# An encoder layer on one core: tiles 0 to 3 turned with a lag of two, norms issued behind a duo's splits, the latents' sums in other buffers and without GpSimd

## The chip, the core and the metric

The kernel runs on one core of a Trainium2 chip. A core has five engines with a queue each: PE (TensorE, the matrix engine), DVE (VectorE), ACT (ScalarE), POOL (GpSimd) and SP, which only issues DMAs here. An engine works through its queue in order; instructions of different engines wait for each other by semaphores. The metric is the device time of one execution in microseconds (us), less is better. The kernel before takes 2342.51 us, the median of three runs (2338.19 to 2344.05).

## The reference, cut to what matters

One layer over 1024 tokens of width 1024, in float32, with four layer norms (LN1 to LN4):

```
x  <- LN1(a*x + 0.5*SwiGLU_1(x))
proj = x @ w_in      -> q_lat (384), kv_lat (256), k_rope (32), u (512), gates g_a, g_b
y_a = attention(q = rms_norm(q_lat) w_uq, k, v = rms_norm(kv_lat) w_uk, w_uv) w_o_attn
y_b = (z * sigmoid(z w_glu)) w_o_ssm,   z = gelu(s5_forward(u) + s5_backward(u) + d*u)
x  <- LN2(a*x + (sigmoid(g_a)*y_a + sigmoid(g_b)*y_b) w_out)
x  <- LN3(a*x + 0.5*SwiGLU_2(x))
x  <- LN4(a*x + sigmoid(x w_pg) * (p w_pp))

rms_norm(t, g) = t * rsqrt(mean(t*t) + 1e-6) * g
layer_norm(t)  = (t - mean) * rsqrt(var + 1e-5) * g + b
SwiGLU(x)      = (silu(x w1) * (x w3)) w2,  w1, w3: 1024 x 2816, w2: 2816 x 1024
```

## The kernel before, in words

**Precision and splits.** A float32 product is made of three matmuls of a shorter type: each operand is split into a high part `hi` (ACT copies and rounds, line 64) and a low part `lo = x - hi` (DVE subtracts, line 65), and hi*hi, hi*lo and lo*hi are added in PSUM. So nearly every operand of PE costs one ACT copy and then one DVE subtraction, in this order (`split`). Names ending in hi, h and lo, l are such halves.

**Feed-forward down (`ffn_down`).** The product with w2 is a block scheme of seven stages; the last is stage 4. A stage goes through the 22 chunks of w2 in six *duos* (two chunks, the last has one). For a duo the hidden values (`hh`, `hl`) and the weights (`wh`, `wl`) are split, then PE does 24 matmuls of 128x512 into four accumulators `pd` (line 441), four for each of the six pairs (rows of token tile t, 128 tokens each). Token tiles 0 to 3 are complete before stage 4 starts, and their layer norm is done within it: in the duo with q = 1 to 4 the generator yields tile q-1 after that duo's splits are written in the program. Tiles 4 to 7 are complete after the last duo.

**Norm and turn (`norm_in`, `layer_norm`, `transpose_in`).** Each yielded tile is normed (ACT: a Square over 128x1024 into `scr`, line 123, and a Sqrt, line 125; DVE: eight 128x1 operations, lines 120 to 130, and two of 128x1024 on `acc`, lines 133 and 135). When more than `lag` normed tiles are waiting, the oldest is turned: eight 128x128 transposes on PE into `tln` (line 148), then a split into `xhi`, `xlo`. `finish` turns those left over. The lag is 4 for LN1 and LN3 and 4 (with blocks) for LN2. After LN1 comes the product with w_u (`pu`), whose moving operand is four turned tiles wide; after LN3 comes the gate of the last layer norm (`pgate`), one tile at a time.

**Latents (`latents`).** Chunks 0 to 2 (q) and 3, 4 (kv) of x w_lat are squared (ACT, line 617), added (DVE, line 619), split, and summed over partitions by a matmul with ones (`pms`, lines 624 and 625), for two halves of 512 tokens. DVE and ACT make the root and its reciprocal (627, 629, 630), and four POOL operations of 128x512 refine it (a Newton step, lines 631 to 634). That is done four times (two groups, two halves). The 128x512 scratch tiles carry the tags t0 to t3, Xr and Xi of the S5 branch's pool; S5's parameter chain on POOL and DVE (line 1104, tiles of 128x32 and their multiples) uses the slots of t2, t3 and Xr too. PE meanwhile does the gates' projection (`pg`).

**Behind S5.** The latents come back from memory (`lat`), POOL multiplies them by the reciprocal root (line 858), ACT scales by the gain and rounds (859), and DVE makes the low part (860) into `ckl` and `mx`. Beside it run the gated linear unit of S5 (`pglu`, `sg`, `sl`), and then the keys (`pk`) and queries (`pq`).

**Order.** The program is written as one list; a scheduler places each engine's instructions by their dependences and buffers, so an edit at one place can reorder an engine's queue around it. `tc.issue_after(x)` binds what is issued in it behind instruction x. Buffers are slots of a tag: a tile whose slot is still in use waits for the last user.

## Time and profile before

| | |
|---|---|
| median of three runs | 2342.51 us |
| profiled execution, its own time | 2340.56 us |
| its span, first to last instruction | 2338.7 us |
| PE busy | 2260.9 us, 97% |
| DVE busy | 1547.1 us, 66% |
| ACT busy | 968.9 us, 41% |
| POOL busy | 269.5 us, 12% |

The profile shows one execution. PE is busy for 97% of the span, so the span less PE's busy time, 77.8 us, is what all its waits, the start and the tail together take. A matmul of 128x512 follows the one before in 0.23 us at a granted clock of 2.4 GHz, and in 0.43 us where the throttle grants 1.2 GHz; a matmul's own duration is longer, since they overlap. A row of the timeline reads: start, duration, engine, line, operation, output <- inputs, shape, count, and in brackets the idle time of that engine just before it with what ended it.

### The profile page before, as it was taken

To read this page: it belongs to the slowest core of one execution; us is meant where nothing else is said; L and a number is where in the kernel's file an instruction comes from. 1 tells how busy PE (TensorE), PEld (TensorE's weight loads), DVE (VectorE), ACT (ScalarE), POOL (GpSimd) and SP (SyncE) were. 2 spreads that over 40 slices of the span, in tenths; PEclk is the share of its full clock that TensorE was granted. 3 is DMA by queue.
4 is the path that set the end of the run, shared out by engine and by line. 5 is a ranking of instruction groups with operands and counts; after the bars stand their busy time and mean duration, and the time that the engine had idled before them with its cause. 6 is when DMAs were issued, how large, how long until landed. Compare 5 with 4: busy or idle time off the path is not lost.

```text
span 2338.7 us, 28503 instructions
## 1 busy us (share of the span) xinstructions
PE 2260.9 (97%) x10784; PEld 1862.5 (80%) x10784; DVE 1547.1 (66%) x2416; ACT 968.9 (41%) x1417; POOL 269.5 (12%) x339
## 2 busy tenths in 40 slices
PE   8999999999989799998999999999999999999998
PEld 7888888877768688886788887788888888777776
DVE  7555656666655698948688876585655656755936
ACT  5333333333432244444478772234333333333525
POOL 0000000000003720004255452100000000000000
PEclk9999999999999899999999999999999999999999
DMA  4323333834234233335200116022323336643301
GB/s 158 112 92 111 106 97 109 302 134 158 94 141 137 81 97 97 90 123 225 74 10 19 37 73 222 31 99 77 123 85 113 101 111 214 226 145 108 131 10 72
DMA packets 104474, 265.63 MB, mean 114 GB/s; under 512 B 13328, under 2 KB 27920, under 8 KB 104336
## 3 DMA queue, kind: packets, MB, share of 16 engines
q1 hardware_dynamic: 104336, 263.80, 33.1%
q8 instruction: 85, 1.39, 0.2%
q14 instruction: 53, 0.43, 0.1%
HBM read 189.33 MB, written 74.42 MB: 113 GB/s over the span
## 4 chain that ended last, share of the span: by engine, by line
PE 48%; DVE 4%; ACT 2%; issue 1%; DMA 0%; POOL 0%; SPq 0%; DVEq 0%; ACTq 0%
PE px L235 9%; PE py L235 5%; PE pd L441 4%; PE pdy L441 4%; PE pd L86 3%; PE pgate L86 3%; PE ps L86 3%; PE pz L235 2%; PE pov L746 2%; PE tpp L733 2%; PE pya L86 2%; PE pyb L86 2%; PE pq L86 1%; PE pu L273 1%; PE pg L273 1%; PE pg L86 1%
## 5 line engine op out<-in xcount | busy, mean ns | idle before, releaser
L65 DVE TENSOR_TENSOR wlo<-raw,whi 128x1024 fp32r<-128x1024 f32 (+4 forms) x116 | 139.0, 1203 | 64.6 <-ACT whi L64 61.9
L64 ACT ACTIVATE whi<-raw 128x1024 fp32r<-128x1024 f32 (+4 forms) x116 | 112.1, 973 | 148.2 <-PE pg L86 70.0
L441 PE MATMUL pd<-wl,hh 128*128 128x512 f32 x352 | 140.1, 398 | 6.0 <-DVE wl L65 6.0
L86 PE MATMUL pg<-xhi,whi 128*128 128x512 f32 x352 | 139.0, 395 | 0.0
L441 PE MATMUL pd<-wh,hl 128*128 128x512 f32 x352 | 138.9, 394 | 0.0
L86 PE MATMUL pg<-xlo,whi 128*128 128x512 f32 x352 | 138.5, 394 | 0.0
L86 PE MATMUL pg<-xhi,wlo 128*128 128x512 f32 x352 | 138.4, 393 | 0.0
L64 ACT ACTIVATE wh<-w2w 128x1024 fp32r<-128x1024 f32 x56 | 59.3, 1058 | 164.8 <-PE pd L441 82.9
L441 PE MATMUL pd<-wh,hh 128*128 128x512 f32 x352 | 120.3, 397 | 0.9 <-ACT wh L64 0.9
L235 PE MATMUL py<-tch,fhl 128*128 128x512 f32 x320 | 106.0, 392 | 0.0
L441 PE MATMUL pdy<-wl,hh 128*128 128x512 f32 x264 | 104.4, 395 | 0.8 <-DVE wl L65 0.8
L441 PE MATMUL pdy<-wh,hl 128*128 128x512 f32 x264 | 104.1, 394 | 0.0
L65 DVE TENSOR_TENSOR hl<-raw,hh 128x1024 fp32r<-128x1024 f32 x84 | 94.6, 1130 | 9.1 <-ACT hh L64 9.1
L64 ACT ACTIVATE fhl<-raw 128x512 fp32r<-128x512 f32 x40 | 25.3, 633 | 180.0 <-PE px L235 177.3
L441 PE MATMUL pdy<-wh,hh 128*128 128x512 f32 x264 | 99.0, 395 | 0.0
L235 PE MATMUL px<-td,thi 128*128 128x512 f32 x320 | 98.8, 390 | 0.0
L65 DVE TENSOR_TENSOR pt<-tpp,pt 128x512 fp32r<-128x512 f32 x128 | 85.6, 684 | 11.9 <-ACT pt L64 10.1
L249 DVE TENSOR_TENSOR c<-raw 128x512 f32<-128x512 f32 x40 | 27.5, 688 | 93.9 <-PE px L235 93.9
L65 DVE TENSOR_TENSOR wl<-w2w,wh 128x1024 fp32r<-128x1024 f32 x56 | 68.3, 1220 | 32.0 <-ACT wh L64 32.0
L720 POOL TENSOR_SCALAR P<-P,sm 128x1024 f32<-128x1024 f32 x64 | 74.7, 1167 | 115.1 <-DVE sm L719 97.3
L86 PE MATMUL ps<-k,qh 96*128 96x512 f32 (+1 forms) x256 | 84.3, 408 | 3.2 <-ACT P L718 1.8
L441 PEld LDWEIGHTS pd<-wl,hh 128*128 128x128 f32 x352 | 66.3, 188 | 24.1 <-DVE wl L65 9.1
(439 smaller groups left out, 6303.0 us busy)
## 6 DMA issues: line engine op xcount, KB each, us to landing
raw<-in_ffn_w_dram SPq DMA_DIRECT2D x86, 512.0 KB, 3.7
raw<-hd SPq DMA_DIRECT2D x70, 512.0 KB, 3.3
hd<-c SPq DMA_DIRECT2D x88, 256.0 KB, 3.5
w2w<-in_ffn_w_dram SPq DMA_DIRECT2D x32, 512.0 KB, 6.3
hd<-s SPq DMA_DIRECT2D x60, 256.0 KB, 3.3
rawx<-in_xT_dram SPq DMA_DIRECT2D x16, 256.0 KB, 6.4
w2e<-in_ffn_w_dram SPq DMA_DIRECT2D x8, 512.0 KB, 8.0
acc<-in_x_dram SPq DMA_DIRECT2D x8, 512.0 KB, 6.3
```

Of the source, the lines that this page charges most:

```text
L64: S.activation(hi, src, AF.Copy)
L65: V.tensor_tensor(out=lo, in0=src, in1=hi.bitcast(F32), op=ALU.subtract)
L86: PE.matmul(out, lhsT=a, rhs=b, start=(n == 0), stop=(n == last))
L235: PE.matmul(out, lhsT=x[:, ks], rhs=y[:, k, :], start=(first and n == 0), stop=(n == 11), skip_group_check=True)
L249: V.tensor_tensor(out=c[:, r], in0=r2[:, l], in1=r2[:, r], op=ALU.add)
L273: PE.matmul(o, lhsT=x[:, ks], rhs=b[y][:, k, :], start=(i == 0 and k == 0 and m == 0), stop=(i == 1 and k == 3 and m == 2), skip_group_che ...
L441: PE.matmul(P[t], lhsT=x[:, ts], rhs=y[:, ws], start=(fresh and p + a == 0 and m == 0), stop=(p + a == NP - 1 and m == 2), skip_group_chec ...
L720: G.tensor_scalar(out=P, in0=P, scalar1=sm, scalar2=1.0, op0=ALU.mult, op1=ALU.mult)
L733: PE.transpose(tp[:, k * 128:k * 128 + 128], P[:, (q * 4 + k) * 128:(q * 4 + k) * 128 + 128], idt)
L746: PE.matmul(p[:, 0:256], lhsT=vt[:, k, c0:c0 + 128], rhs=pt[k // 4][b][:, k % 4, :], start=(k == 0 and b == 0), stop=(k == 7 and b == 1))
```

## The change

Three groups of edits:

1. **Norms and turns.** `split` returns its two instructions. In stage 4 the layer norm of tiles 0 to 3 is bound behind the two instructions that split the duo's weights (`issue_after`). Inside the loop only tiles 0 to 3 are turned, the lag falls from 4 to 2 for LN1 and LN3 and from 4 to 3 for LN2.
2. **Latents' sums.** The scratch tiles take the tags WTr, WTi and M, two slots each, in place of t0 to t3, Xr and Xi; the four Newton operations go from POOL to DVE, four times.
3. **Scaling of the latents.** POOL's product and ACT's scaling become one DVE operation (lat * gain * reciprocal root), followed by a plain split.

POOL issues 21 instructions less, DVE 21 more, ACT two more (loads of its function table), PE as many as before.

```diff
     def split(src, hi, lo):
-        S.activation(hi, src, AF.Copy)
-        V.tensor_tensor(out=lo, in0=src, in1=hi.bitcast(F32), op=ALU.subtract)
+        a = S.activation(hi, src, AF.Copy)
+        return a, V.tensor_tensor(out=lo, in0=src, in1=hi.bitcast(F32), op=ALU.subtract)
...
         for j, sums in steps:
-            layer_norm(acc[j], sums, gt, bt, pool)
+            with ExitStack() as after:
+                for i in behind_splits:
+                    after.enter_context(tc.issue_after(i.ins))
+                layer_norm(acc[j], sums, gt, bt, pool)
             ready.append(j)
-            if len(ready) > lag:
+            if len(ready) > lag and ready[0] < 4:
                 bring(False)
...
-                split(w, *[t[:, 0:n * 512].rearrange("p (a b) -> p a b", a=n) for t in (wh, wl)])
+                last = split(w, *[t[:, 0:n * 512].rearrange("p (a b) -> p a b", a=n) for t in (wh, wl)])
                 held.append((p, n, hh, hl, wh, wl))
                 if i == 4 and 0 < q < 5:
+                    behind_splits[:] = last
                     yield q - 1, sums[q - 1]
+                    behind_splits.clear()
...
-        finish = norm_in(chain([first], dn), acc, *ln, x1T, fp, spill, 4)
+        finish = norm_in(chain([first], dn), acc, *ln, x1T, fp, spill, 2)
...
-        def t(tag, dt=F32):
-            return tp.tile([128, 512], dt, tag=tag, name="r" + tag)
+        def t(i, dt=F32):
+            return tp.tile([128, 512], dt, tag=("WTr", "WTi", "M")[i], bufs=2, name="r")
...
-                hi, lo = t(f"t{2 + h}", F32R), t(("Xr", "Xi")[h], F32R)
+                hi, lo = t(1, F32R), t(2, F32R)
...
-                G.tensor_tensor(out=s, in0=y, in1=y, op=ALU.mult)
-                G.tensor_tensor(out=s, in0=s, in1=v, op=ALU.mult)
-                G.tensor_scalar(out=s, in0=s, scalar1=-0.5, scalar2=1.5, op0=ALU.mult, op1=ALU.add)
-                G.tensor_tensor(out=y, in0=y, in1=s, op=ALU.mult)
+                V.tensor_tensor(out=s, in0=y, in1=y, op=ALU.mult)
+                V.tensor_tensor(out=s, in0=s, in1=v, op=ALU.mult)
+                V.tensor_scalar(out=s, in0=s, scalar1=-0.5, scalar2=1.5, op0=ALU.mult, op1=ALU.add)
+                V.tensor_tensor(out=y, in0=y, in1=s, op=ALU.mult)
...
-            G.tensor_tensor(out=lat[i], in0=lat[i], in1=rstd[i], op=ALU.mult)
-            S.activation(hi, lat[i], AF.Copy, scale=g)
-            V.scalar_tensor_tensor(out=lo, in0=lat[i], scalar=g, in1=hi.bitcast(F32),
-                                   op0=ALU.mult, op1=ALU.subtract)
+            V.scalar_tensor_tensor(out=lat[i], in0=lat[i], scalar=g, in1=rstd[i], op0=ALU.mult, op1=ALU.mult)
+            split(lat[i], hi, lo)
...
-        finish = norm_in(chain([first], steps), acc, gt, bt, X2, fp, store, 4, True)
+        finish = norm_in(chain([first], steps), acc, gt, bt, X2, fp, store, 3, True)
...
-    finish = norm_in(chain([first], dn), acc, gt, bt, x3T, fp, lag=4)
+    finish = norm_in(chain([first], dn), acc, gt, bt, x3T, fp, lag=2)
```

**The order at three places, all on DVE.** Lines in the changed kernel are 5 to 7 higher than before (441 is 448, 133 stays, 617 to 634 are 624 to 641, 858 to 860 become 865 and the split, 1104 is 1109).

First, DVE's queue at the end of the first feed-forward's stage 4, up to the low half of tile 3 (xlo from tln_4631 before, tln_4577 now; w_u's weights are `wlo`). Before:

```order
L65 TENSOR_TENSOR wlo_4652<-raw_4649,whi_4651 128x1024 [waits DMAHW1_49,Activation_49]
L65 TENSOR_TENSOR wlo_4664<-raw_4661,whi_4663 128x1024 [waits DMAHW6_49,Activation_49]
L124 TENSOR_SCALAR ln2_4538<-ln1_4537 128x1 [waits Activation_49]
L133 SCALAR_TENSOR_TENSOR acc_2999<-acc_2999,ln0_4536,ln_4296 128x1024
L65 TENSOR_TENSOR wlo_4658<-raw_4655,whi_4657 128x1024 [waits DMAHW4_49,Activation_49]
L124 TENSOR_SCALAR ln2_4577<-ln1_4576 128x1 [waits Activation_49]
L133 SCALAR_TENSOR_TENSOR acc_3000<-acc_3000,ln0_4575,ln_4296 128x1024
L65 TENSOR_TENSOR xlo_4301<-tln_4631,xhi_4299 128x8x128 [waits Activation_49]
```

and now:

```order
L65 TENSOR_TENSOR wlo_4652<-raw_4649,whi_4651 128x1024 [waits DMAHW0_49,Activation_49]
L120 TENSOR_SCALAR ln0_4599<-sums_3008 128x1 [waits DVE_49]
L124 TENSOR_SCALAR ln2_4523<-ln1_4522 128x1 [waits Activation_49]
L133 SCALAR_TENSOR_TENSOR acc_2998<-acc_2998,ln0_4521,ln_4296 128x1024
L120 TENSOR_SCALAR ln0_4626<-sums_3009 128x1 [waits DVE_49]
L65 TENSOR_TENSOR wlo_4664<-raw_4661,whi_4663 128x1024 [waits DMAHW3_49,Activation_49]
L65 TENSOR_TENSOR wlo_4658<-raw_4655,whi_4657 128x1024 [waits DMAHW1_49,Activation_49]
L65 TENSOR_TENSOR xlo_4301<-tln_4538,xhi_4299 128x8x128 [waits Activation_49]
L124 TENSOR_SCALAR ln2_4562<-ln1_4561 128x1 [waits Activation_49]
L133 SCALAR_TENSOR_TENSOR acc_2999<-acc_2999,ln0_4560,ln_4296 128x1024
L65 TENSOR_TENSOR xlo_4301<-tln_4577,xhi_4299 128x8x128 [waits Activation_49]
```

From wlo_4652 to tile 3's low half there stood three weight halves, two norm products and that half; now there stand three weight halves, two norm products and the halves of tiles 2 and 3.

Second, DVE's queue in the latents, from S5's Vr to the low half of a sum (the operand of `pms`: rXr_5439 before, where r_5457 is the sum behind it now; Cw needs POOL's T2r). Before:

```order
L1104 TENSOR_TENSOR v1_5844<-PV1_4964,c_re_4957 128x512 [waits DVE_49]
L1104 TENSOR_TENSOR Vi_5847<-Vi_5847,v1_5844 128x512 [waits DVE_49]
L1104 TENSOR_TENSOR Cw_5786<-T2r_4969,T1r_4967 128x512 [waits Pool_49]
L1104 TENSOR_TENSOR Sw_5787<-T2r_4969,T1i_4968 128x512
L1104 TENSOR_TENSOR v1_5844<-PW1_4966,bb_im_4962 128x512 [waits DVE_49]
L1104 TENSOR_TENSOR v2_5727<-T2i_4970,T1i_4968 128x512 [waits Pool_49]
L65 TENSOR_TENSOR rXr_5439<-rt0_5248,rt2_5438 128x512 [waits Pool_49]
```

and now:

```order
L634 TENSOR_SCALAR r_5445<-pms_5442 128x512 [waits PE_49]
L1109 TENSOR_TENSOR v1_5844<-PV1_4964,c_im_4959 128x512 [waits DVE_49]
L1109 TENSOR_TENSOR Vr_5846<-Vr_5846,v1_5844 128x512 [waits DVE_49]
L637 RECIPROCAL r_5447<-r_5446 128x512 [waits Activation_49]
L1109 TENSOR_TENSOR Cw_5786<-T2r_4969,T1r_4967 128x512 [waits Pool_49]
L1109 TENSOR_TENSOR Sw_5787<-T2r_4969,T1i_4968 128x512
L65 TENSOR_TENSOR r_5457<-r_5249,r_5456 128x512 [waits Activation_49]
L1109 TENSOR_TENSOR v1_5844<-PV1_4964,c_re_4957 128x512 [waits DVE_49]
```

The low half of the first sum now stands eight rows ahead of this piece, and its reciprocal within it; the low half of the second sum, which stood behind the first's, now stands two rows behind Cw. In PE's queue the first sum's second matmul (line 625, now 632) has moved ahead by 44 matmuls of the gates, and the second sum's now stands where twelve more gate matmuls and two more of the sums have been done than before the first sum's in the kernel before.

Third, DVE's queue where the latents are scaled, with the linear unit's `sg` and `sl`. Before:

```order
L849 TENSOR_TENSOR sg_7930<-sg_7930,zT_7845 128x512 [waits Activation_49]
L849 TENSOR_TENSOR sg_7948<-sg_7948,zT_7847 128x512 [waits DMAHW6_49,Activation_49]
L65 TENSOR_TENSOR sl_7825<-sg_7930,sh_7824 128x512 [waits Activation_49]
L65 TENSOR_TENSOR sl_7825<-sg_7948,sh_7824 128x512 [waits Activation_49]
L860 SCALAR_TENSOR_TENSOR ckl_8007<-lat_7853,gq_7829,mx_8005 128x1024 [waits DMAHW3_49,Activation_49]
L860 SCALAR_TENSOR_TENSOR ckl_8007<-lat_7855,gq_7829,mx_8006 128x1024 [waits Activation_49]
```

and now:

```order
L865 SCALAR_TENSOR_TENSOR lat_7853<-lat_7853,gq_7829,rms_7851 128x1024 [waits DMAHW3_49,DMAHW1_49,DMAHW0_49]
L856 TENSOR_TENSOR sg_7930<-sg_7930,zT_7845 128x512 [waits Activation_49]
L856 TENSOR_TENSOR sg_7948<-sg_7948,zT_7847 128x512 [waits DMAHW6_49,Activation_49]
L865 SCALAR_TENSOR_TENSOR lat_7855<-lat_7855,gq_7829,rms_7851 128x1024 [waits DMAHW2_49]
L65 TENSOR_TENSOR ckl_8007<-lat_7853,mx_8005 128x1024 [waits Activation_49]
L65 TENSOR_TENSOR sl_7825<-sg_7930,sh_7824 128x512 [waits Activation_49]
L65 TENSOR_TENSOR sl_7825<-sg_7948,sh_7824 128x512 [waits Activation_49]
L865 SCALAR_TENSOR_TENSOR lat_7859<-lat_7859,gq_7829,rms_7857 128x1024 [waits DMAHW4_49,DMAHW3_49]
L65 TENSOR_TENSOR ckl_8007<-lat_7855,mx_8006 128x1024 [waits Activation_49]
```

The products that POOL made stand in DVE's queue now, and the first `ckl` has moved ahead of both `sl`.

## Rows read from the trace of the kernel before

**Rows 1.** The page's first part: busy time of each engine in us, its share of the span, and instructions.

```profile
PE 2260.9 (97%) x10784; PEld 1862.5 (80%) x10784; DVE 1547.1 (66%) x2416; ACT 968.9 (41%) x1417; POOL 269.5 (12%) x339
```

**Rows 2.** PE's waits over the whole span: engine, tile and line that waited <- what ended it; us in total, times, longest.

```profile
PE pms L625 <- DVE rXr L65: 12.3, 1, 12.3
...
PE pk L86 <- DVE ckl L860: 6.2, 1, 6.2
PE pd L441 <- DVE wl L65: 6.0, 6, 2.0
```

**Rows 3.** Three stretches around PE's long waits: us from the span's start, length, busy us (instructions) of PE, weight loads, DVE, ACT and POOL, then the granted clock of PE as a share of 2.4 GHz, DMA share and GB/s.

```profile
668.00:680.00 12.00, 6.96 (x18) 5.19 (x19) 12.00 (x33) 4.12 (x10) 0.00 (x0) 0.57 0.56 189
784.00:799.00 15.00, 6.13 (x16) 4.70 (x17) 9.64 (x15) 5.40 (x7) 7.66 (x24) 0.54 0.11 43
1070.00:1079.00 9.00, 4.67 (x13) 3.72 (x14) 9.00 (x6) 2.41 (x4) 7.44 (x4) 0.62 0.00 0
```

**Rows 4.** PE's timeline in stage 4 of the first feed-forward: where duo 1's matmuls end and duo 2's begin, and the last transposes with the start of w_u's product.

```profile
633.14 0.40 PE L441 MATMUL pdy<-wh,hl 128*128 128x512 f32 x1
634.01 1.06 PE L148 MATMUL tln<-idt,acc 128*128 128x128 f32 x8 [0.47 <-DVE ln L124]
635.00 1.20 PE L441 MATMUL pd<-wh,hh 128*128 128x512 f32 x4
638.17 0.50 PE L441 MATMUL pd<-wl,hh 128*128 128x512 f32 x1 [1.98 <-DVE wl L65]
...
670.56 0.79 PE L86 MATMUL pu<-xhi,whi 128*128 128x512 f32 x1 [5.29 <-ACT xhi L64]
673.84 0.79 PE L86 MATMUL pu<-xlo,whi 128*128 128x512 f32 x1 [2.49 <-DVE xlo L65]
```

**Rows 5.** PE's timeline at the same step of an earlier stage of the second feed-forward, where no norm stands in between.

```profile
2111.49 1.19 PE L441 MATMUL pd<-wh,hh 128*128 128x512 f32 x4 [0.23 <-ACT wh L64]
2113.18 0.50 PE L441 MATMUL pd<-wl,hh 128*128 128x512 f32 x1 [0.50 <-DVE wl L65]
```

**Rows 6.** ACT's and then DVE's timeline between the last transposes and w_u's product.

```profile
667.42 1.04 ACT L64 ACTIVATE whi<-raw 128x1024 fp32r<-128x1024 f32 x1
668.37 1.13 ACT L123 ACTIVATE scr<-acc,ln 128x1024 bf16<-128x1024 f32 x1
...
666.65 2.35 DVE L65 TENSOR_TENSOR wlo<-raw,whi 128x1024 fp32r<-128x1024 f32 x2
...
671.37 1.27 DVE L133 SCALAR_TENSOR_TENSOR acc<-acc,ln,ln 128x1024 f32<-128x1024 f32 x1
672.57 1.22 DVE L65 TENSOR_TENSOR xlo<-tln,xhi 128x1024 fp32r<-128x1024 f32 x1
```

**Rows 7.** The timelines of PE, DVE and ACT in the latents, around PE's longest wait.

```profile
780.13 0.39 PE L86 MATMUL pg<-xhi,wlo 128*128 128x512 f32 x1
792.87 0.80 PE L625 MATMUL pms<-rXr,ones 128*128 128x512 f32 x1 [12.35 <-DVE rXr L65]
...
788.94 0.72 DVE L1104 TENSOR_TENSOR Cw<-T2r,T1r 128x512 f32<-128x512 f32 x1 [13.18 <-POOL T2r L1104]
789.58 0.90 DVE L1104 TENSOR_TENSOR Sw<-T2r,T1i 128x512 f32<-128x512 f32 x1
792.13 0.68 DVE L65 TENSOR_TENSOR rXr<-rt,rt 128x512 fp32r<-128x512 f32 x1
...
791.69 0.63 ACT L617 ACTIVATE rt<-og 128x512 f32<-128x512 f32 x1 [21.44 <-POOL Xr L1104]
```

**Rows 8.** DVE behind it: the reciprocal, one operation of S5 without and with a POOL operation beside it, and a stretch of 10 us (columns as in rows 3).

```profile
798.92 3.35 DVE L630 RECIPROCAL rXr<-rt 128x512 f32<-128x512 f32 x1
822.20 0.63 DVE L1104 TENSOR_TENSOR Wr<-PW,bb_re 128x512 f32<-128x512 f32 x1
832.83 1.69 DVE L1104 TENSOR_TENSOR Wr<-PW,bb_re 128x512 f32<-128x512 f32 x1
...
810.00:820.00 10.00, 10.00 (x50) 8.29 (x49) 4.83 (x6) 4.36 (x7) 2.85 (x2) 1.00 0.44 134
```

**Rows 9.** Where the latents are scaled: POOL, DVE and PE, and from the view of the tile `lat` the time from its loads' issue (the first at 1053.6 us) to landing.

```profile
1062.14 14.36 POOL L858 TENSOR_TENSOR lat<-lat,rms 128x1024 f32<-128x1024 f32 x5 [61.40 <-DVE wlo L65]
...
1065.35 5.65 DVE L65 TENSOR_TENSOR sl<-sg,sh 128x512 fp32r<-128x512 f32 x2
1070.91 6.67 DVE L860 SCALAR_TENSOR_TENSOR ckl<-lat,gq,mx 128x1024 fp32r<-128x1024 f32 x2
1078.71 1.27 DVE L860 SCALAR_TENSOR_TENSOR mx<-lat,gq,mx 128x1024 fp32r<-128x1024 f32 x1
...
1067.52 0.61 PE L86 MATMUL pk<-mx,whi 128*128 128x512 f32 x2
1074.33 0.80 PE L86 MATMUL pk<-ckl,whi 128*128 128x512 f32 x1 [6.20 <-DVE ckl L860]
...
DMA to landing us min/median/max: 8.3/10.6/10.6
```

**Rows 10.** The start of the gate behind the second feed-forward, on PE, and a table load on ACT.

```profile
2205.33 0.47 PE L86 MATMUL pgate<-whi,xhi 128*128 128x512 f32 x1
2210.09 0.50 PE L86 MATMUL pgate<-wlo,xhi 128*128 128x512 f32 x1 [2.23 <-DVE wlo L65]
...
2215.15 1.28 ACT L1052 ACT_TABLE_LOAD   x1
```

More of the change, by code (lines that the diff above doesn't have):

```diff
@@ L183, in differences @@
         V.tensor_tensor(out=b21, in0=b21, in1=b11, op=ALU.subtract)
+    behind_splits = []
     def norm_in(steps, acc, gt, bt, xT, pool, done=None, lag=3, blocks=False):
@@ L606, in latents @@
         G.memset(ones.bitcast(F32), 1.0)
-        def t(tag, dt=F32):
-            return tp.tile([128, 512], dt, tag=tag, name="r" + tag)
+        def t(i, dt=F32):
+            return tp.tile([128, 512], dt, tag=("WTr", "WTi", "M")[i], bufs=2, name="r")
         for i, (m0, n) in enumerate(((0, 3), (3, 2))):
-            tot = [t("t0"), t("t1")]
+            tot = [t(0), t(0)]
             for m in range(m0, m0 + n):
@@ L615, in latents @@
                 for h in range(2):
-                    sq = tot[h] if m == m0 else t(f"t{2 + h}")
+                    sq = tot[h] if m == m0 else t(1)
                     S.activation(sq, o[:, h * 512:h * 512 + 512], AF.Square)
@@ L625, in latents @@
                 PE.matmul(p, lhsT=ones, rhs=lo, start=False, stop=True)
-                v, s, y = t(f"t{h}"), t(f"t{2 + h}"), t(("Xr", "Xi")[h])
+                v, s, y = t(0), t(1), t(2)
                 V.tensor_scalar(out=v, in0=p, scalar1=1.0 / (128 * n), scalar2=RMS_EPS,
```

## The prediction

> **What bounds the kernel now.** I read the page's first part first: PE is busy for 97% of the span [rows 1], so nothing that the other engines save counts unless PE waits for it, and 2338.7 - 2260.9 = 77.8 us is the most that could go. Second, PE's waits: two single ones, 12.3 us for a latents' sum and 6.2 us for `ckl`, and six of `pd` on `wl` [rows 2]. Third, the granted clock: behind each long wait PE runs at 1.2 GHz for a while, the mean around the three being 0.57, 0.54 and 0.62 [rows 3]. Fourth, the timelines at these places [rows 4, 6, 7, 9, 10]. The change touches four places where PE waits; elsewhere PE is fed, so a gain at one of them is kept to the end, unless a later wait takes it.
>
> **Place 1, the end of the first feed-forward.** Before, between duo 1's last matmul (633.14 + 0.23 = 633.37) and the first `pd<-wl` of duo 2 (638.17) lie 4.8 us [rows 4]: eight transposes (0.99), four matmuls, and waits of 0.47 and 1.98 us, the latter since the splits of duo 2 stand behind the norms in DVE's queue. With the splits ahead, the step should look as it does where there is no norm: waits of 0.23 and 0.50 us around four matmuls [rows 5], from 2111.49 - 0.23 to 2113.18, about 1.9 us, so `pd<-wl` starts at about 635.4. From then to the last `pd` two tiles are turned, as before (tiles 0 and 1 now, 1 and 2 then), so the last `pd` ends 2.75 us earlier, at about 661.5. But now two tiles are still to be turned (before: one), and `pu` needs the low halves of all four. DVE decides: before, from the first `wlo` (666.65) it made three weight halves, two norm products and tile 3's half, to 672.57 + 1.22 = 673.8, when PE resumed [rows 4, 6]. Now its first `wlo` comes at 666.65 - 2.75 + 1.2 (tile 3's last norm product, which the order puts ahead of it) = 665.1; then follow, by the order, three weight halves, two norm products and two tiles' halves, seven operations of 1.15 to 1.2 net of overlap (1.22 and 1.27 in the rows), 8.2 us: 673.3. ACT is not late: from 661.5 three `whi` (1.04), two squares (1.13) and two `xhi` give 669. So **-0.5 us** of the 2.75 stay; the idle time and the half clock behind it remain. Bounds: -2.8 if DVE is not the limit, +2.5 if both turned tiles come one whole split (1.2 + 1.2) later. In SP's queue the stores of x1 and w_u's loads change places; the weights' first use is far behind.
>
> **Place 2, the latents.** Before, PE stops at 780.13 + 0.23 and resumes at 792.87, for the low half of the first sum [rows 7]. Two things held it: ACT's square waited 21.4 us for POOL's Xr, whose slot it shared, and DVE stood 13.2 us at Cw, which waits for POOL's T2r, until 788.94. The new buffers remove the first: the first sum goes through long before Cw. They don't remove the second: in the order the second sum's low half stands behind Cw and Sw. Sw runs from 789.58 for 0.90, so the half starts at about 790.4 and takes 0.68: PE resumes at about 791.2. Until it stops it can now do twelve gate matmuls and two of the sums more, 14 x 0.23 = 3.2 us, so it idles from 783.6, for 7.6 us. The half clock behind the wait stays: a mean of 0.54 over 15 us [rows 3] is 13.8 us at half, to about 798, so some 5 us of work at 0.43 in place of 0.23 us a matmul, 2.4 us lost, before and now. The gain is 12.35 - 7.6 = 4.7, of which I count **-4.2 us**, with half a microsecond for the sums' matmuls that stand in smaller gaps now. POOL's T chain itself is not shortened. DVE gets 4 x (three of 0.68 and one of 0.63) = 10.7 us of Newton steps, not shown on DVE in the trace, but 128x512 as the operations whose durations I take [rows 7, 8]. Their cover: one reciprocal of 3.35 us moves into DVE's 13 us of waiting, DVE is idle for 5.2 of 10 us between 810 and 820, and S5's operations, which took up to 1.69 us beside POOL's Newton step, should take 0.63 again [rows 8]. If that cover is gone, the cost is 10.7 less the slowdowns. I take these three as paying for the 10.7 and count nothing. Bounds of the place: -14.7 (the wait and its half clock vanish) and +6.5 (no cover at all: 10.7 - 4.2).
>
> The row of 1.69 us stands beside POOL's Newton step, that of 0.63 does not [rows 8]. The Trainium skill ("SBUF — State Buffer", "Who interferes with whom") says that a DVE operation with two SBUF inputs and a GpSimd operation that reads SBUF exclude each other, the later one waiting for the earlier one's end. By that rule the slowdowns go with POOL's steps, and the place gives the -4.2; if they came from something else that stays, the 10.7 less 3.35 and 5.2 would cost 2.2 us and the place would give -2. The trace agrees with the rule as far as the two rows go, so I stay with -4.2.
>
> **Place 3, scaling the latents.** Before, POOL's five products take from 1062.14 to 1076.5; beside them DVE's two `sl` take 5.65 us for a pair and the two `ckl` 6.67, against 1.27 for the same operation alone later; PE reaches `pk` at 1067.52 and waits 6.2 us [rows 9]. Now DVE multiplies itself: from about 1062.1 (the first latent's load, issued at 1053.6, lands 8.3 us later [rows 9], and POOL started then) lat 1.27, two `sg` 0.69 each, lat 1.27, `ckl` 1.2: done at 1067.3, before PE needs it at 1068. Two `sl`, lat, second `ckl`: 1071.1, PE needs it at about 1073. The queries' operand is next late: three products and two `sg` more put its low half at 1076.2, where PE, 28 matmuls further (6.5 us), is at 1074.0: a new wait of 2.2 us. So 6.2 - 2.2 = 4.0, and the half clock goes too, if 2.2 us of waiting don't bring it back (a mean of 0.62 over 9 us is 6.8 us at half, 3.7 of them with PE at work from 1074.3 to 1078, so nine matmuls of 0.43 in place of 0.23: 1.8 us): **-6 us**, rounded up by 0.2. Bounds: -8 (no new wait), -2 (the new wait is 4 us, its half clock returns).
>
> **Place 4, the end of the second feed-forward.** The same 2.75 us less 1.0 for the transposes that move behind: -1.7 at the last `pd`. The gate takes one tile at a time, so it starts with tile 0, whose halves are long made: it starts at about 2203.1 in place of 2205.33, but its second slab's low half (`wlo`) again comes late behind the four evictions of `pd`, at about 2207.4 in place of 2210.09 [rows 10]. Then the two kernels run alike, with a half-clock stretch in both. The order shows two more table loads on ACT, around the first sigmoid, 1.28 each [rows 10]. Walked through the order with these durations, that sigmoid ends at about 2218.2, behind the squares and norm products of tiles 4 to 7, and the third tile, which needs its bank, starts at 2220.6. So the loads are hidden, with 2.4 us to spare. **-2 us**; bounds -4.5 and +3.
>
> LN2's lag (4 to 3) hardly moves anything in the order: 0.
>
> **Sum.** -0.5 - 4.2 - 6 - 2 = -12.7. From the profiled execution's 2340.56 that is 2327.9; the median of the runs lies 1.95 above that execution, so 2329.8, say **2330 us**.
>
> **Rivals.**
> (a) *The latents' wait goes whole.* If the scheduler's order binds less than it looks, or T2r comes earlier because POOL's chain shares nothing with DVE any more, PE never stops there: -14.7 in place of -4.2, so 2319. For it: the removed wait on Xr is the longest of the page. Against it: Cw's wait on T2r is as long, and it is in front of the second sum.
> (b) *The waits only move.* The second sum waits for Cw and later ones for the Newton steps, tiles 2 and 3 are turned as late as the weights, and the queries wait in place of the keys: places 1, 2 and 4 give nothing, place 3 gives 2 or 3 us. 2340. For it: in all four places I found a next wait close behind.
> (c) *Slower: DVE's queue in the latents.* Each of the three later sums' low halves now stands on DVE behind a reciprocal of 3.35 and Newton steps of 2.7. If PE waits for each of them by that 6 us, with the half clock behind each (2.4 as after the first), that is 8.4 us a sum; from two of them on (16.8) it exceeds the other gains, with three it is 25.2 - 12.7 = +12.5: 2355. For it: DVE is the engine that gets work. Against it: PE has 77 gate matmuls, 18 us, between the second and the third sum, and DVE idles there.
>
> **How the numbers follow.** A difference under 0.3% (7 us) can't be told from none for this kernel. My forecast 2330 (own range 2322 to 2336): 0.56; (a) 0.14; (b) 0.20; (c) 0.10. The range for 8 in 10 takes in all but the ends of (a) and (c): 2316 to 2343. Faster than 2335.5: 0.92 of the forecast and (a), and a tenth of (b): 0.67; within 0.3%: the rest of these, 0.23; slower: (c), 0.10.
>
> **What would show it.** Right: `pms` waits once, 7 to 8 us, ended by a low half behind Cw; `pk` doesn't wait for `ckl`, a wait of some 2 us stands at `pq`; no wait of 2 us of `pd` on `wl` in the duos with norms; `pu` waits about as long as before, `pgate` about 2.5 us. Wrong: S5's first scan waited for by PE; DVE full from 800 to 850 with PE waiting; the half clock at new places.

## The result and the profile after

The changed kernel takes 2327.65 us (median of 4 runs, 2326.62 to 2328.71), the kernel before, on the same chip, 2342.66: a ratio of 0.9939 with an interval of 0.9922 to 0.9956. That is 15 us faster, and the forecast was 2330. In the profiled executions the span falls by 11.9 us, from 2338.7 to 2326.8.

The page's first part answers to [rows 1]: PE works as long as before, so the time came from its waits.

```profile
PE 2260.3 (97%) x10784; PEld 1863.0 (80%) x10784; DVE 1543.6 (66%) x2437; ACT 971.1 (42%) x1419; POOL 233.9 (10%) x318
```

PE's waits over the whole span [rows 2]:

```profile
PE pms L632 <- DVE r L65: 7.5, 1, 7.5
PE pu L86 <- DVE ln L124: 7.5, 2, 6.0
...
PE py L1397 <- ACT Xr L1387: 6.5, 1, 6.5
PE pd L448 <- DVE wl L65: 3.1, 6, 0.5
...
PE pq L86 <- DVE mx L65: 1.6, 1, 1.6
```

The latents' wait (`pms`) is 7.5 us in place of 12.3, the keys' 6.2 us are gone with 1.6 in their place at `pq`, and `pd` lost its waits of 2 us. But `py` is new, a wait of 6.5 us in a place that the change doesn't touch: the last read-out of S5. In the kernel before, PE's wait there is:

```profile
PE py L1392 <- ACT Xi L1382: 0.8, 1, 0.8
```

To sum this up with the half-clock stretches in it, I took for each pair of successive matmuls the time from start to start, less the median of such times for the same line and shape, and added up these differences, in us:

| stretch, us | place | before | after | change | forecast |
|---|---|---|---|---|---|
| 600-700 | 1, end of the first feed-forward | 15.1 | 13.3 | -1.8 | -0.5 |
| 750-850 | 2, latents | 18.4 | 10.1 | -8.4 | -4.2 |
| 1000-1050 | last block of S5 | 1.7 | 11.8 | **+10.0** | none |
| 1050-1150 | 3, scaling | 16.4 | 10.3 | -6.1 | -6 |
| 2150-2250 | 4, end of the second feed-forward | 11.1 | 5.3 | -5.8 | -2 |
| whole span | | 105.9 | 94.0 | -12.0 | -12.7 |

**Place 1** [rows 4, 6], PE and then DVE:

```profile
635.97 0.50 PE L448 MATMUL pd<-wl,hh 128*128 128x512 f32 x1 [0.52 <-DVE wl L65]
...
661.99 1.91 PE L148 MATMUL tln<-idt,acc 128*128 128x128 f32 x16
669.85 0.76 PE L86 MATMUL pu<-xhi,whi 128*128 128x512 f32 x1 [5.95 <-DVE ln L124]
672.14 0.79 PE L86 MATMUL pu<-xlo,whi 128*128 128x512 f32 x1 [1.53 <-DVE ln L124]
...
663.57 1.22 DVE L65 TENSOR_TENSOR wlo<-raw,whi 128x1024 fp32r<-128x1024 f32 x1
...
668.48 1.22 DVE L65 TENSOR_TENSOR xlo<-tln,xhi 128x1024 fp32r<-128x1024 f32 x1
...
670.87 1.22 DVE L65 TENSOR_TENSOR xlo<-tln,xhi 128x1024 fp32r<-128x1024 f32 x1
```

Two tiles' transposes stand behind the last `pd`, `pu` waits for both halves of tile 3, and goes on at 672.14 (before: 673.84).

**Place 2** [rows 7]: the wait, and DVE's queue that ends it.

```profile
781.81 0.39 PE L86 MATMUL pg<-xhi,wlo 128*128 128x512 f32 x1
789.68 0.79 PE L632 MATMUL pms<-r,ones 128*128 128x512 f32 x1 [7.49 <-DVE r L65]
...
787.43 0.72 DVE L1109 TENSOR_TENSOR Cw<-T2r,T1r 128x512 f32<-128x512 f32 x1 [8.77 <-POOL T2r L1109]
788.07 0.90 DVE L1109 TENSOR_TENSOR Sw<-T2r,T1i 128x512 f32<-128x512 f32 x1
788.89 0.73 DVE L65 TENSOR_TENSOR r<-r 128x512 fp32r<-128x512 f32 x1
```

**The last block of S5.** S5 goes through eight blocks. For each, PE makes sums (`pe`, line 1361), DVE scans them (20 operations), ACT turns the result round (`Xr`, `Xi`), and PE reads out (`py`). While a block's scan runs, PE does matmuls of the gates (`pg`), 14 projections of 48 in the loop; two more are bound behind the last read-out. PE's timeline in the changed kernel:

```profile
1010.28 0.39 PE L86 MATMUL pg<-xhi,wlo 128*128 128x512 f32 x1
1011.23 0.46 PE L1395 MATMUL py<-U,M 128*128 128x128 f32 x2 [0.56 <-issue]
1018.19 0.80 PE L1397 MATMUL py<-Xr,Vr 128*128 128x128 f32 x2 [6.51 <-ACT Xr L1387]
1019.49 0.80 PE L1397 MATMUL py<-Xi,Vi 128*128 128x128 f32 x2 [0.49 <-ACT Xi L1387]
```

Windows (columns as in rows 3) of the gates' matmuls alone, from 700 us to the first sums of S5 and from the last sums to the end of the read-out (this one for PE alone); before:

```profile
700.00:824.80 124.80, 82.94 (x349) 66.96 (x349) 0.00 (x0) 7.12 (x7) 0.95 0.34 109
...
1009.00:1025.00 16.00, 10.14 (x43) 1.00 0.17 36
```

and after:

```profile
700.00:825.10 125.10, 89.71 (x383) 72.96 (x383) 0.00 (x0) 7.09 (x7) 0.97 0.35 112
...
1005.00:1025.00 20.00, 4.69 (x17) 0.75 0.25 66
```

S5's first sums start at the same time (824.8 and 825.1), with 34 matmuls of the gates more done: the time won in the latents went into gates. At the end they are missing: 43 of them covered the last scan, now 17 (by the program's order, from the last sums to the first read-out, 41 and 14). In between PE never stops, and DVE is not far from full:

```profile
850.00:900.00 50.00, 50.00 (x285) 42.63 (x284) 44.92 (x80) 22.17 (x33) 0.42 (x4) 1.00 0.30 90
...
950.00:1000.00 50.00, 50.00 (x311) 42.95 (x311) 43.92 (x80) 22.25 (x36) 0.42 (x4) 1.00 0.39 117
...
1018.00:1025.00 7.00, 6.31 (x25) 5.83 (x26) 0.00 (x0) 2.20 (x4) 0.00 (x0) 0.50 0.01 2
```

The last row is what follows the wait: 7 us at 0.50, the level of 1.2 GHz.

A smaller part of the new wait is DVE's own. In the changed kernel the low half of a weight stands in the midst of the last scan, where before it comes behind it (at 1023.26 us):

```profile
1013.75 1.22 DVE L65 TENSOR_TENSOR wlo<-raw,whi 128x1024 fp32r<-128x1024 f32 x1
```

From the start of the last sums to the end of the last of ACT's copies it is 14.1 us here and 13.0 us in the kernel before.

**Place 3** [rows 9]: `pk` waits 0.9 us, `pq` 1.6, and the clock stays up.

```profile
1064.29 1.28 DVE L865 SCALAR_TENSOR_TENSOR lat<-lat,gq,rms 128x1024 f32<-128x1024 f32 x1 [2.24 <-DMA rms<-rmsd]
...
1069.16 0.50 PE L86 MATMUL pk<-ckl,whi 128*128 128x512 f32 x1 [0.94 <-DVE ckl L65]
...
1077.43 0.50 PE L86 MATMUL pq<-mx,whi 128*128 128x512 f32 x1 [1.57 <-DVE mx L65]
...
1066.00:1078.00 12.00, 9.31 (x39) 6.72 (x38) 12.00 (x14) 9.15 (x13) 0.94 (x1) 1.00 0.55 207
```

**Place 4** [rows 10]: the low half of the gate's second slab stands right behind DVE's four evictions, where before three norm products and the half of a tile stood among and behind them (2203.19 to 2208.7 us). It comes in time, and no half clock follows.

```profile
2195.90 1.04 PE L148 MATMUL tln<-idt,acc 128*128 128x128 f32 x8
2196.69 0.48 PE L86 MATMUL pgate<-whi,xhi 128*128 128x512 f32 x1
...
2198.85 0.50 PE L86 MATMUL pgate<-wlo,xhi 128*128 128x512 f32 x1 [0.28 <-DVE wlo L65]
...
2195.08 0.69 DVE L392 SCALAR_TENSOR_TENSOR acc<-acc,pd 128x512 f32<-128x512 f32 x1
...
2197.57 1.23 DVE L65 TENSOR_TENSOR wlo<-raw,whi 128x1024 fp32r<-128x1024 f32 x1
...
2195.00:2215.00 20.00, 19.72 (x94) 15.97 (x93) 19.29 (x51) 16.00 (x23) 0.00 (x0) 1.00 0.44 149
```

### The profile page after: what moved, and what is told of

It is laid out like the page before. It is cut to its first block, busy times and chain, and to the rows that moved or that the text cites. A ratio compares the mean times of both kernels' runs of the same rounds, so it can differ in the third digit from the quotient of the medians.

```text
span 2326.8 us, 28503 instructions
## 1 busy us (share of the span) xinstructions
PE 2260.3 (97%) x10784; PEld 1863.0 (80%) x10784; DVE 1543.6 (66%) x2437; ACT 971.1 (42%) x1419; POOL 233.9 (10%) x318
## 4 chain that ended last, share of the span: by engine, by line
PE 47%; DVE 5%; ACT 2%; issue 1%; DMA 1%; SPq 0%; POOL 0%; DVEq 0%; ACTq 0%; POOLq 0%
PE px L240 9%; PE py L240 5%; PE pdy L448 4%; PE pd L86 4%; PE pd L448 3%; PE pgate L86 3%; PE ps L86 3%; PE pz L240 2%; PE pov L753 2%; PE tpp L740 2%; PE pya L86 2%; PE pyb L86 2%; PE pq L86 1%; PE pg L86 1%; PE pu L278 1%
## 5 line engine op out<-in xcount | busy, mean ns | idle before, releaser
L65 DVE TENSOR_TENSOR pt<-tpp,pt 128x512 fp32r<-128x512 f32 x128 | 85.6, 685 | 11.6 <-ACT pt L64 10.3
```

What stands on the lines that cost most here:

```text
L65: return a, V.tensor_tensor(out=lo, in0=src, in1=hi.bitcast(F32), op=ALU.subtract)
```

## The experiments

The kernel before ran beside each group of these kernels, with medians of 2340.82 to 2342.66 us. The ratios are taken against it; a time given as below or above the changed kernel compares medians of different groups, so that some 2 us of it can't be told from nothing.

**Each part alone.** The change's hunks one group at a time, on the kernel before.

```diff
 e1: split() returns its instructions; layer_norm bound behind_splits; ready[0] < 4; lags 2, 3, 2
 e2: tags WTr, WTi, M in latents(); G.tensor_tensor -> V.tensor_tensor for Newton's step
 e3: V.scalar_tensor_tensor(out=lat[i], ...) and split(lat[i], hi, lo) for the latents
```

> Only the first part of the change: turns with a lag of two or three, none for tiles 4 to 7 inside the loop, norms tied behind the splits; latents and scaling as before. Theory (the trace's windows add up, place by place): 1.7 us at the end of FFN1 and 5.8 us at the end of FFN2, so about 7 us below the kernel before, ratio 0.997, with PE resuming near 672 us and the gate starting near 2201 us at full clock. Rival (most of the gain comes from the latents and the scaling, and the two FFN ends only shift a wait): within 2 us of before, ratio 0.999 to 1.000.

Measured: 2334.53 us, ratio 0.9970 (0.9959 to 0.9981), 6.3 us below the kernel before: the theory's size.

> Only the latents' part: sums in other buffers, Newton's step on VectorE. Theory (what the latents win comes back at the last scan of S5, because the matmuls of the gates that stood there are used up earlier): 8.4 us won by 850 us, about 10 us lost at 1000 to 1024 us, so level with before or up to 3 us slower, ratio 0.999 to 1.001, with a wait of 6 us or more at the last read-out. Rival (the wait at the last scan has nothing to do with the latents and comes from the norms or from the scaling): 6 to 8 us faster, ratio 0.997, and the last read-out waits under 1 us as in the kernel before.

Measured: 2339.66 us, ratio 0.9991 (0.9982 to 0.9999). The wait stands at the last read-out as in the full change:

```profile
PE py L1392 <- ACT Xr L1382: 6.6, 1, 6.6
```

By the same sum as in the table above, this kernel wins 8.6 us in the latents and loses 10.1 in S5's last block. So the rival falls: the new wait is the latents' own doing. That the kernel is 1.2 us faster all the same comes from elsewhere: 4.7 us at the end of the second feed-forward, which this kernel doesn't touch in its source. The scheduler had put the four evictions there in another order, and the gate's wait of 2.2 us was gone.

> Only the scaling of the latents without GpSimd. Theory (each place stands alone): 6 us below the kernel before, ratio 0.9975, no half clock between 1060 and 1080 us, a wait of 2 us at the first query projection. Rival (the scaling's wait only shows because the latents came late, so it gives nothing alone): ratio 0.999 to 1.000.

Measured: 2334.02 us, ratio 0.9967 (0.9956 to 0.9979), 6.8 us below the kernel before: the theory, though the first query projection waits 0.9 us, not 2. The three differences to before, 6.3, 1.2 and 6.8 us, make 14.3, the full change 15.0: within the noise the parts add up.

**How many gates are left for the last scan.** First, the same work, with the loop's last gate kept for that place.

```diff
     for t in range(8):
-        next(step)
+        last = next(step)          # the last sums (pe) of scan t
         for _ in range(1 if t in (0, 7) else 2):
-            project(sp, [gates.pop(0)])
+            with ExitStack() as after:
+                if t == 7:
+                    after.enter_context(tc.issue_after(last.ins))
+                project(sp, [gates.pop(0)])
```

> The changed kernel with the last gate of the S5 loop tied on TensorE behind the sums of the last scan, so that 48 gate matmuls instead of 14 stand between these sums and the last read-out, and 8 fewer pieces before. The amount of work is the same. Theory A (the order of the program spends the gates too early): the wait of 6.5 us at the last read-out falls to under 2 us, the half clock behind it goes, 6 to 9 us below the changed kernel, about 2320 us. Theory B (VectorE's chain of scans sets when S5 ends, the gates only fill): the wait moves to the read-out or the transposes before it, 0 to 2 us below the changed kernel, about 2326 us.

Measured: 2322.96 us, ratio 0.9920 (0.9907 to 0.9933), 4.7 us below the changed kernel with no run in common: between the two theories. The wait at the read-out is gone, and one stands at the transposes of the block before, which now has too few gates itself:

```profile
995.81 0.63 PE L1323 MATMUL pw<-idt,Wi 128*128 128x128 f32 x4 [3.84 <-DVE Wi L1112]
```

From that block's sums to the last ones it is 23.1 us in place of 25.2, though 34 gate matmuls (34 x 0.23 = 7.8 us) fewer stand there. So in the loop PE, filled by gates, sets the pace, with DVE's chain only 2 us behind; at the loop's end the chain alone decides.

Second, one of the two gates that stand behind the read-out is allowed in front of it:

```diff
-        for _ in range(1 if t in (0, 7) else 2):
+        for _ in range(2 if t else 1):
             project(sp, [gates.pop(0)])
```

> The changed kernel with 15 of the 16 gates in the S5 loop instead of 14, so that one gate (48 matmuls) that stood behind the last read-out may stand before it: 62 gate matmuls behind the last scan's sums instead of 14, 48 instead of 96 behind the read-out. Theory A (too few gates were left for the last scan, and those behind it cover more than the 12 us in which z goes out, comes back and is split): the wait of 6.5 us at the last read-out and its half clock go, the first GLU matmul waits at most 3 us; 6 to 9 us below the changed kernel, about 2320 us. Theory B (VectorE's chain sets the end of S5, and behind it every gate is needed as cover): the wait moves to z, within 2 us of the changed kernel, about 2327 us.

Measured: 2317.96 us, ratio 0.9896 (0.9876 to 0.9917): A, with 9.7 us below the changed kernel, a little over the 6 to 9 expected. PE doesn't stop in the last block, and 48 gate matmuls behind it are cover enough for z:

```profile
1000.00:1050.00 50.00, 49.28 (x273) 41.15 (x271) 21.83 (x40) 23.54 (x33) 0.00 (x0) 1.00 0.46 144
```

Third, the latents' wait itself. Cw and Sw of the first block are bound on DVE behind the latents' splits (the tie is to the last of the four):

```diff
-        cmul(C_, S_, (x(T2[0]), x(T2[1])), (y(T1[0]), y(T1[1])), g2, V)
+        with ExitStack() as after:
+            if t == 0:
+                after.enter_context(tc.issue_after(lats[0].ins))   # latents() returns its last split
+            cmul(C_, S_, (x(T2[0]), x(T2[1])), (y(T1[0]), y(T1[1])), g2, V)
```

> The changed kernel with the tables Cw and Sw of S5's first block tied on VectorE behind the second latent sum's split, so that the wait of 7.5 us at the latents' sums has nothing to stand behind. Theory A (what TensorE wins before S5 comes back at the last scan, since the gates are spent earlier: no gate is left behind the last sums): the wait at the latents' sums falls under 2 us, that at the last read-out grows from 6.5 to 10 us or more, within 2 us of the changed kernel, about 2327 us. Theory B (the two waits are separate): 6 to 8 us below the changed kernel, about 2320 us.

Measured: 2318.90 us, ratio 0.9905 (0.9887 to 0.9923), 8.8 us below the changed kernel: B. The wait in the latents is gone, PE waits nowhere from 750 to 1000 us, and the read-out waits longer, but only for 9.0 us in two pieces:

```profile
1005.91 0.77 PE L1400 MATMUL py<-U,M 128*128 128x128 f32 x2 [4.39 <-DMA zd<-zo]
1011.30 0.80 PE L1402 MATMUL py<-Xr,Vr 128*128 128x128 f32 x2 [4.63 <-ACT Xr L1392]
```

The profile puts the end of the first piece down to a store of `zo`, but that store was issued only at 1004.13 us; what the matmul reads is `M`, whose eight loads were issued from 1000.43 to 1003.6 us and land some 1.9 us after issue, the last at about 1005.5, so I take it for that. Either way PE had to wait for `Xr` behind it.

My theory A was right in kind and wrong in size. A gain in the latents is paid for by the gates that stood at the end, and only 14 were left there, 14 x 0.23 = 3.2 us. The wait grew by 1.9 us (from 6.51 and 0.56 to 9.02), while the low half of a weight left the last scan, which took 13.0 us in place of 14.1: together 3.0. When the stock is spent, further gains are kept.

> The edits of the two runs beside it together: the tables behind the latents' split, and one gate more in the S5 loop (42 gate matmuls behind the last sums). Theory A (one stock of gate matmuls covers both places): both waits become small only together; about 5 us below the better of the two alone, some 12 us below the changed kernel, about 2315 us. Theory B (VectorE's chain sets the end of S5): no better than the run with one gate earlier alone, a wait of 6 us or more at the last read-out.

Measured: 2310.70 us, ratio 0.9865 (0.9840 to 0.9889), 17 us below the changed kernel, more than A's 12: the read-out waits 0.8 us, as before the change, with 42 gate matmuls in front of it. B falls. But A's "only together" falls too: each edit alone had ended the wait that it was made for, and the two gains, 9.7 and 8.8 us, nearly add up to the 17.

These kernels give a rule of thumb for this place. From the start of the last sums to the last of ACT's copies it is 13.0 to 14.6 us, of which PE's own sums and first products take some 3, so by my estimate some 43 to 50 gate matmuls of 0.23 us are wanted in this loop. With 62, 48 or 42 of them the wait is none, none or 0.8 us, with 30 (Newton's step on GpSimd, below) 4.2, with 14 it is 6.5, with none 9.0.

**Newton's step.** Back on GpSimd, with the new buffers, and then left out.

```diff
 e8: -                V.tensor_tensor(out=s, in0=y, in1=y, op=ALU.mult)   (and the three behind it)
     +                G.tensor_tensor(out=s, in0=y, in1=y, op=ALU.mult)
 e11: the four operations removed
```

> The changed kernel with Newton's four products back on GpSimd, the new buffers kept. Theory A (the new buffers alone ended the waits in the latents, VectorE has room for Newton's 10.7 us): within 2 us of the changed kernel, the wait at the latents' sums 7 to 8 us as there, VectorE's operations beside GpSimd's long again at 780 to 830 us. Theory B (GpSimd's hold on the buffers and its slower products made the waits): the wait at the latents' sums grows by 2 us or more or the first scans come later, 3 us or more above the changed kernel. Theory C (Newton on VectorE holds up the chain of scans): 2 us or more below.

Measured: 2329.17 us, ratio 0.9943 (0.9925 to 0.9961): no difference that could be told from the changed kernel, A in sum. In its parts it has something of B: `pms` waits another 2.5 us at 807, and the read-out, with 30 gate matmuls in front of it, waits 2.3 us less. Beside GpSimd's product DVE's into Wr is long again, here with the one of GpSimd that ends within it, and behind it the same operation in the changed kernel:

```profile
820.52 1.44 DVE L1109 TENSOR_TENSOR Wr<-PW,bb_re 128x512 f32<-128x512 f32 x1 [0.23 <-PE pw L1320]
...
819.29 2.13 POOL L639 TENSOR_TENSOR r<-r 128x512 f32<-128x512 f32 x1
```

```profile
818.56 0.69 DVE L1109 TENSOR_TENSOR Wr<-PW,bb_re 128x512 f32<-128x512 f32 x1
```

> The changed kernel without Newton's steps on the reciprocal square roots: 16 operations of VectorE, 10.7 us, are left out. Theory A (they run in VectorE's idle time and TensorE is fed by the gates meanwhile, as the forecast counted): within 1.5 us of the changed kernel, the waits at the latents' sums and at the last read-out as there, 7.5 and 6.5 us. Theory B (they push the scans back): 4 us or more below the changed kernel, the wait at the last read-out shorter by as much.

Measured: 2313.96 us, ratio 0.9881 (0.9868 to 0.9895), 13.7 us below: B, and not what I expected. The wait in the latents is about as it was, 7.1 us; PE is full from 800 to 1000 in both kernels; but S5's first sums come 7.6 us earlier (817.5), and 48 gate matmuls are left for the last scan, so that nothing waits there:

```profile
1000.00:1050.00 50.00, 48.44 (x226) 39.91 (x224) 20.20 (x36) 21.54 (x31) 0.00 (x0) 1.00 0.48 168
```

So Newton's steps (9.8 us on DVE in the profile, where 10.7 were forecast) are covered by gates, and the cover is paid for 200 us later: by the same sum as above 9.7 of the 13.7 us come from S5's last block. Another 1.6 are the waits of `pk` and `pq`, which fall from 2.5 to 0.9 us. With the steps on GpSimd (e8) the kernel is no faster, so in the changed kernel it is the steps that cost this, not their move. What they cost in the kernel before was not run; there the last read-out waits only 0.8 us, so there was little to win at that place.

**The tie and the lags.** One of the two taken out of the changed kernel.

```diff
 e9:  -                    behind_splits[:] = last
 e10: lags back to 4, 4, 4 and "and ready[0] < 4" removed, the tie kept
```

> The changed kernel without the tie of the norms behind a duo's splits, the turns' new lags kept. Theory A (the tie ends the 2 us waits of the second layer's matmuls for the low half of the weights, once in each feed-forward, and with them the late start of the last duos): both waits return, 3 to 5 us above the changed kernel, about 2331 us, the gate's wait for its second low half at 2 us or more again. Theory B (the lags make the gain): at most 1 us above.

Measured: 2322.53 us, ratio 0.9921 (0.9908 to 0.9933), 5.1 us *below* the changed kernel; both theories fall as to the time. The waits of 2 us are back at both feed-forwards, as A said, but the whole idle time behind the first is gone:

```profile
638.01 0.50 PE L447 MATMUL pd<-wl,hh 128*128 128x512 f32 x1 [1.98 <-DVE wl L65]
...
664.72 0.40 PE L447 MATMUL pd<-wh,hl 128*128 128x512 f32 x1
664.95 0.39 PE L86 MATMUL pu<-xhi,whi 128*128 128x512 f32 x1
```

The last transposes ahead of `pu` stand at 660.53, among the last duo's matmuls, and `pu` follows `pd` with no gap. The next rows are the window from 660 to 680 us, in this kernel and, in the fence behind it, in the changed one:

```profile
660.00:680.00 20.00, 20.00 (x90) 16.41 (x90) 18.77 (x48) 10.25 (x18) 0.00 (x0) 1.00 0.45 163
```

```profile
660.00:680.00 20.00, 12.52 (x51) 9.79 (x50) 20.00 (x51) 9.88 (x17) 0.00 (x0) 0.74 0.42 150
```

> The changed kernel with the turns' lags as before (four, and tiles 4 to 7 turned inside the loop too), the tie kept. Theory A (the tie makes the gain at the two feed-forwards): at most 2 us above the changed kernel, the gate's wait for its second low half under 1 us as there. Theory B (the lags make the larger part at the second feed-forward, since with them no transposes and no halves of a tile stand among the last splits): 3 to 5 us above, about 2332 us, the gate's wait at 2 us or more.

Measured: 2327.45 us, ratio 0.9940 (0.9927 to 0.9954), theory A: with the tie, the lags do nothing. Without the tie a short lag brings all four tiles' turns into the duos (e9, the last at 660.53 us). With it two tiles' transposes stand behind the last `pd` at either lag, at 661.43 us here and at 661.99 in the changed kernel, so that the lag has nothing to win. In the first feed-forward the tie wins 1.9 us and costs 9.4. In the second, where the gate takes one tile at a time and needn't wait for four, the tie wins 2.6.

**A version from these.** Both S5 edits, and the tie in the second feed-forward alone (`behind_splits[:] = last if tied else []`, with `tied` set before the third `norm_in`).

> The kernel of the run with both S5 edits (tables behind the latents' split, one gate more in the loop), with the norms tied behind the splits in the second feed-forward only. Theory (the tie and the lag work against each other at the end of the first feed-forward and not at the second, and the places are independent): the idle time of some 9 us behind the first feed-forward goes, its 2 us wait of duo 2 comes back, 7 to 8 us below that run's 2310.7 us: about 2303 us, ratio 0.9835. Rival (the gain at the first feed-forward only moves into the latents, which then wait for GpSimd's tables or for S5's chain): 2308 us or more.

Measured: 2300.30 us (2299.64 to 2303.12), ratio 0.9827 (0.9814 to 0.9841), 27 us below the changed kernel: the theory, with 10.4 us below e7 in place of 7 to 8. Its longest waits are the start of the program and one of 2 us:

```profile
PE pu L278 <- ACT xah L64: 7.0, 3, 5.4
PE pd L448 <- DVE wl L65: 4.0, 5, 2.0
```

The same sum over PE as above, for all kernels (us lost in the stretches of the first table, without the rest):

| kernel | median, us | FFN1 end | latents | S5's last block | scaling | FFN2 end |
|---|---|---|---|---|---|---|
| changed | 2327.7 | 13.3 | 10.1 | 11.8 | 10.3 | 5.3 |
| e1 norms only | 2334.5 | 12.9 | 18.3 | 1.7 | 17.9 | 5.2 |
| e2 latents only | 2339.7 | 15.6 | 9.8 | 11.8 | 16.0 | 6.4 |
| e3 scaling only | 2334.0 | 15.9 | 18.6 | 1.7 | 8.7 | 11.3 |
| e4 gate held | 2323.0 | 13.2 | 10.1 | 1.5 | 9.3 | 5.4 |
| e5 one gate earlier | 2318.0 | 13.6 | 10.1 | 1.9 | 10.6 | 5.5 |
| e6 latents first | 2318.9 | 13.8 | 1.3 | 13.3 | 8.6 | 5.6 |
| e7 both | 2310.7 | 13.1 | 1.4 | 5.5 | 9.7 | 5.7 |
| e8 Newton on GpSimd | 2329.2 | 13.5 | 15.3 | 7.6 | 9.7 | 5.3 |
| e9 no tie | 2322.5 | 5.8 | 10.2 | 12.4 | 9.0 | 7.9 |
| e10 old lags | 2327.5 | 13.2 | 9.6 | 11.7 | 9.8 | 5.4 |
| e11 no Newton | 2314.0 | 13.2 | 9.9 | 2.1 | 6.7 | 5.6 |
| e12 combined | 2300.3 | 5.7 | 1.3 | 7.2 | 5.1 | 4.0 |

In e7 and e12 everything comes earlier, so that a part of the scaling falls into the column of S5's last block.

## Why the prediction was right, and where it was not

**The time and its parts.** 2330 was forecast, 2327.65 came. The parts were further off than the sum: three places gave 9.3 us more than forecast (1.3, 4.2 and 3.8), and 10.0 us came back at a place that the forecast doesn't name. The agreement of the sum is in part luck.

**Place 2, and the step that failed.** The wait itself was forecast to a tenth of a microsecond: 7.6 us behind Cw, measured 7.5, once, ended by the low half behind Cw and Sw. The gain at the place was 8.4 us where 4.2 were forecast, for two reasons that the runs show: the half clock behind the wait, counted as 2.4 us "before and now", is shorter (from 792 to 800 us the mean clock is 0.93, before 0.62, so that by my estimate it ends some 3.5 us behind the wait, before 5.2), and PE's 2.1 us of idle time between 800 and 850 went as well. What failed is the sentence "elsewhere PE is fed, so a gain at one of them is kept to the end, unless a later wait takes it". I looked for that later wait only among the latents' sums. PE was fed by the gates, these are a stock, and the order showed before the run that 34 more of them stand ahead of S5 and 27 fewer at its end. The runs with the latents alone, with one gate earlier and without Newton's step show it. With the latents alone the kernel won 1.2 us, and that only with the 4.7 us at the end of the second feed-forward; in the latents and S5's last block together it lost 1.5 us (-8.6 and +10.1), where -4.2 were forecast.

**Newton on DVE counted at nothing.** Right as a cost of moving: with it on GpSimd the time is the same within the intervals. Beside POOL's Newton step the product into Wr took 1.44 us, in the changed kernel 0.69. The Trainium skill ("SBUF — State Buffer", "Who interferes with whom") has the two engines exclude each other there, and these two rows agree with it. The pair in the prediction was read too simply: the product of 0.63 us at 822.20 also has an operation of POOL beside it, which began 0.17 us later and took 1.36 us, where the same one at 802.40 took 1.04. So there the later one was POOL's. The cover, however, is not free as "count nothing" had it: e11 shows that the kernel without the steps is 13.7 us faster, 9.7 of them in S5's last block, by way of the gates.

**Place 1.** Forecast -0.5, measured -1.8, PE back at 672.14 for 673.3: the first `wlo` came at 663.57, not 665.1, since tile 3's last norm product (1.28 us at 661.04) ran ahead of the last two evictions, while `pd` was still at work. The idle time did remain, as forecast. I took it as DVE's due, however, and didn't ask what the tie and the lag would do apart: e9 and e10 show that they work against each other here: with the lag alone 9.3 us are won at this place (15.1 to 5.8).

**Place 3.** Forecast -6, measured -6.1, alone 6.8. `pk` waits 0.9 us, where I had none, since the reciprocal root landed 2.2 us later than I took; `pq` waits 1.6 for 2.2; no half clock.

**Place 4.** Forecast -2, measured -5.8. The term that was off is the gate's wait for its second low half: I left it at about 2.5 us, behind four evictions, with a half clock. In the new order the low half comes right behind these evictions, the wait is 0.28 us, and the half clock never comes. In e1, e2 and e10 the wait is 0.3 us or none too, in e9 0.9, in e3 still 2.2. Since e2 doesn't touch this place, no edit of the place is needed for it: the scheduler's order makes it. The two table loads were hidden, as counted.

**The rivals.** (a) asked for T2r earlier, which came at 787.4 and not much before; e6 shows what it would have been worth, 8.8 us. (b), the waits only move, is the mechanism that was in fact at work, for 10 us, not with its places. (c) didn't come: no later sum waits.

## What to carry to other kernels

Work that fills an engine's waits is a stock: a wait that it covers is not free, it is paid for where the stock runs out, if it does, so count the filler on both sides of an order before crediting a gain, and look first at the end of the loop that it fills. Here one gate moved across the last read-out, which is no faster work at all, was worth as much as two thirds of the whole change. And two edits that each help may oppose each other: take each out alone before keeping both.

## What was not expected

- An edit in the latents at 780 us removed 4.7 us at 2200 us, in code that it doesn't touch, by way of the scheduler's order alone (e2). A single edit's effect can't be read from its place alone.
- PE's clock after a stop: behind the wait of 6.5 us it stood at 0.50 for 7 us, behind that of 1.57 us at 1.00 (1077 to 1085 us). In e4, behind a wait of 3.84 us, the mean was 0.72 from 995.8 to 1002 us and 1.00 from 1002 to 1008.
- A load of ACT's function table took 1.28 us and the next operation followed at once: the load at 2207.52 us, the sigmoid at 2208.81, as the rows of the changed kernel show.

```profile
2207.52 1.28 ACT L1057 ACT_TABLE_LOAD   x1 [0.88 <-PE pgate L86]
2208.81 0.60 ACT L1057 ACTIVATE gs<-pgate 128x512 f32<-128x512 f32 x1
```
